# The latent attention's four projection tiles computed inside the loop over the directions' tables, and the shift's centre term from PSUM on ScalarE

## The chip, the cores and the metric

The kernel runs on one core of one Trainium2 chip. The metric is the time of one execution on the device in microseconds (us); lower is better. Engines: TensorE (PE in the profile; PEld is its weight load), VectorE (DVE), ScalarE (ACT), GpSimd (POOL) and SyncE (SP), which here only starts DMAs. ScalarE starts DMAs too.

## The reference, cut to what matters

The model is two hybrid layers (latent attention beside a bidirectional recurrence, then a mixture of experts) and a third block of another kind. Only the projection of the two hybrid layers is touched. For each layer li, on L = 1040 tokens (16 of them meta tokens) of width 1024:

```python
proj = h @ w_in[li]                                   # 1024 -> 448 + 1920 columns
c_q, c_kv, k_pe, rw = _split(proj, [256, 128, 64, 1920])
y_att = _mla(c_q, c_kv, k_pe, cos, sin, ...)          # rms norms of c_q and c_kv, rotation of k_pe
u = _centred_shift(rw, mu_prev, mu_next)              # p + mu_prev*(prev - p) + mu_next*(next - p)
r, k, v, wd_f, wd_b, ad_f, ad_b, gd = _split(u, [512, 512, 512, 64, 64, 64, 64, 128])
v = v + (v_first - v) * sigmoid(v0 + (v @ v1) @ v2)   # the second layer only
g = sigmoid(gd) @ g2
kk = k * k_k / sqrt(sum over a head of (k*k_k)**2 + 1e-12)
# per direction d: decay = exp(-exp(-softplus(-(w0 + tanh(wd) @ w2)) - 0.5)),
#                  a = sigmoid(a0 + ad @ a2),  kd = k * (1 + (a - 1) * k_a)
y_f, y_b = the recurrence over tokens of (r, decay, kd, v, kk, a), forward and reversed
```

## The kernel before, in words

**Tiles.** `proj` (L346) works with features on the 128 partitions and tokens along the free axis. One feature tile is 128 columns of `w_in` for all tokens (1040, padded to 1044). There are 19: fifteen of the recurrence (four of r, four of k, four of v, one each for wd, ad and gd), each of which goes through the centred shift, and four of the latent attention (two of c_q, one of c_kv, one of k_pe with its rotated copy), which do not. `ftile` makes one: it loads the weights (`load`, L357, on SyncE's queue), splits them into a high and a low part (ScalarE L251, VectorE L252), and issues 72 matmuls (three thirds of the tokens, eight pieces of the contraction, three products of the split, L256 to L258) into one PSUM buffer of three banks.

**Buffers.** PSUM has eight banks: the pool tag `mm` has two buffers of three banks each, the tag `tp` two of one bank. Projection tiles and the low-rank products of the loop both take `mm`; the transposes, the gate's products, the sums for the bonus and the sums of squares take `tp`. The weights' tiles, the evicted tile `pt` and the shifted tile `u` have two buffers each in SBUF.

**The shift.** `shifted` (L386 to L393) evicts the PSUM buffer with one ScalarE copy into `pt` (L390), multiplies by the centre coefficient on VectorE (L391), and adds the two neighbours with two more VectorE instructions (L392, L393). `plain` (L441, in `latent`) evicts without a shift (L444).

**Order.** The stage runs: the wd and ad tiles; `dirs`, which takes the four k tiles, forms the unit keys, and then loops over f = 0 to 3 (each: one r tile, then for both directions the decay and the gate of the keys from low-rank products L563, a scan L573, exponentials L576 and L577, and the products that fill two tables, AR and BK, L590 to L607, stored to DRAM at L610 from ScalarE's queue; then the sums for the bonus, L616). Behind the loop come the four v tiles, `values` (the residual of the second layer, L657 to L671; then for the forward and the reversed order of tokens nine transposes each, L684, a ScalarE copy L686 and a store L687), and `latent`: the rotated key, the gate's tile gd and its nine products, the key-value tile with its norm (reciprocal L495), the two q tiles, whose squares are summed over the features by 36 small matmuls (L513) for the rms norm. The products of other tiles are woven in by the `mid` hooks, called after a given third of a tile.

The kernel's instructions are put in order on each engine by a planner: it takes what is ready by its own model of the times, the earlier in the program first, and hands out buffers as they come free. Engines then run their queues in that order. DMAs signal through a small set of semaphores that are used in turn, so that a DMA can also wait for an earlier one with the same semaphore.

After the projection the recurrence `recur` starts: `r_fetch` loads pieces of AR and BK (L810, SyncE) and the first products are L825.

Of the kernel before, what the change touches and what calls it, by code (L numbers as in the profile page):

```python
# [10 lines left out]
F32 = mybir.dt.float32  # L11
# [4 lines left out]
AF = mybir.ActivationFunctionType  # L16
ALU = mybir.AluOpType
# [155 lines left out]
class K:  # L173
# [172 lines left out]
    def proj(self, li, hi, lo, p, S, psp, feed):  # L346

        nc, tc, I = self.nc, self.tc, self.I
        w = I["w_in"][li]
        with self.tpool(name="p_w", bufs=2) as wp, self.tpool(name="p_u", bufs=2) as up, \  # L350
# [34 lines left out]
            def shifted(j, u, mid={}):  # L385

                ps = ftile(own(j), early.pop(j, None), mid)
                pt = up.tile([128, TP + 1], F32, name="pt")
                nc.vector.memset(pt[:, 0:1], 0.0)
                nc.scalar.activation(pt[:, 1:].rearrange("p (q n) -> p q n", q=3), ps, AF.Copy)  # L390
                nc.vector.tensor_scalar(u, pt[:, 1:T + 1], p["c0"][:, j:j + 1], None, ALU.mult)  # L391
                nc.vector.scalar_tensor_tensor(u, pt[:, 0:T], p["mup"][:, j:j + 1], u, ALU.mult, ALU.add)  # L392
                nc.vector.scalar_tensor_tensor(u, pt[:, 2:T + 2], p["mun"][:, j:j + 1], u, ALU.mult, ALU.add)  # L393
                if self.dbg:
                    self.dbg(f"u{li}", (1920, T), u, lambda a: a[128 * j:128 * j + 128])
                return u
# [21 lines left out]

            wd = cp.tile([128, TP], F32, name="s_wd")
            ad = cp.tile([128, TP], F32, name="s_ad")  # L420
            for t in (wd, ad):
                nc.vector.memset(t[:, T:], 0.0)
            u = shifted(12, up.tile([128, T], F32, name="u"))
            nc.scalar.activation(wd[:, :T], u, AF.Tanh)
            shifted(13, ad[:, :T])
            lw = {}
            for nm in ("w2", "a2"):
                lw[nm] = cp.tile([128, RW], F32, name=f"r_{nm}")
                nc.sync.dma_start(lw[nm], I[f"rwkv_{nm}"][li].rearrange("d r f -> (d r) f"))
            with self.tpool(name="p_k", bufs=1) as kp:  # L430
                self.dirs(li, p, S, psp, up, kp, shifted, wd, ad, lw)
            with self.tpool(name="p_v", bufs=1) as vp:
                vt = [shifted(8 + f, vp.tile([128, T], F32, name=f"vt{f}", tag=f"val{f}")) for f in range(4)]
                self.values(li, vt, p, S, psp, up, vp)
                self.latent(li, p, S, psp, up, vp, shifted, ftile)

    def latent(self, li, p, S, psp, up, vp, shifted, ftile):

        nc = self.nc

        def plain(cols, mid=None):  # L441
            ps = ftile(cols, mid={2: mid} if mid else {})
            pt = up.tile([128, TP + 1], F32, name="pt")
            nc.scalar.activation(pt[:, :TP].rearrange("p (q n) -> p q n", q=3), ps, AF.Copy)  # L444
            return pt[:, :T]

        def c3(fn):
# [12 lines left out]
        nc.sync.dma_start(g2, self.I["rwkv_g2"][li])  # L460

        kr = plain([(384, 64, 0), (416, 32, 64), (384, 32, 96)])
        nc.gpsimd.tensor_tensor(kr[:64], kr[:64], cos[:64], ALU.mult)
        nc.gpsimd.tensor_tensor(kr[64:], kr[64:], sin[64:], ALU.mult)

        u = shifted(14, up.tile([128, T], F32, name="u"))
        gd = vp.tile([128, T], F32, name="gd")
        nc.scalar.activation(gd, u, AF.Tanh, scale=0.5)
        nc.vector.tensor_scalar(gd, gd, 0.5, 0.5, ALU.mult, ALU.add)

        def keys_end():
            ps = psp.tile([128, 3, 512], F32, name="kp_ps", tag="mm")
            c3(lambda q, c, n: nc.tensor.matmul(ps[:, q, :n], dup, kr[:, c:c + n], start=True, stop=True))
            b = vp.tile([128, T], F32, name="kp", tag="val3")
            c3(lambda q, c, n: nc.scalar.activation(b[:, c:c + n], ps[:, q, :n], AF.Copy))
            nc.scalar.dma_start(S["ckv"][1], b)


        ck = plain([(256, 128, 0)], keys_end)
        b = vp.tile([128, T], F32, name="ck_sq", tag="val2")  # L480
        nc.scalar.activation(b, ck, AF.Square)

        def gate_end():
            for c, n in TT:
                gp = psp.tile([128, 512], F32, name="g_ps", tag="tp")
                nc.tensor.matmul(gp[:n], gd[:, c:c + n], g2, start=True, stop=True)
                gs = vp.tile([128, RW], F32, name="g_sb", bufs=2)
                nc.scalar.activation(gs[:n], gp[:n], AF.Copy)
                nc.scalar.dma_start(S["g"][c:c + n, :], gs[:n])

        def ckv_end():
# [8 lines left out]
        sq = []  # L500
        for f, mid in enumerate((gate_end, ckv_end)):
            a = plain([(128 * f, 128, 0)], mid)
            x = vp.tile([128, T], F32, name=f"cq_sq{f}", tag=f"val{f}")
            nc.scalar.activation(x, a, AF.Square)
            sq.append(x)
            nc.vector.tensor_scalar(a, a, p["qn"][:, f:f + 1], None, ALU.mult)
            nc.scalar.dma_start(S["cq"][f], a)
        rq, nrq = S["rq"], S["nrq"]
        nc.vector.memset(rq, 1.0)
        sqs = psp.tile([128, 9, 2], F32, name="sqs", tag="tp")  # L510
        for i, (c, n) in enumerate(TT):
            for f in range(2):
                nc.tensor.matmul(sqs[:n, i], sq[f][:, c:c + n], ones[:, 0:2], start=f == 0, stop=f == 1)  # L513
        nc.scalar.activation(rq[:NM, 0:1], sqs[:NM, 0, 0:1], AF.Sqrt, scale=1.0 / 256, bias=self.eps["rms"][:NM])
        nc.scalar.activation(rq[:, 1:9], sqs[:, 1:9, 0], AF.Sqrt, scale=1.0 / 256, bias=self.eps["rms"])
# [4 lines left out]
    def dirs(self, li, p, S, psp, up, kp, shifted, wd, ad, lw):  # L520


        nc = self.nc
# [5 lines left out]
            nc.vector.tensor_scalar(rkp[:, f], self.pair, p["rk"][:, f:f + 1], None, ALU.mult)  # L529
        kt, kkt = [], []  # L530
        for f in range(4):
            k = shifted(4 + f, kp.tile([128, T], F32, name=f"k{f}"))
# [7 lines left out]
        for d in range(2):  # L540
            nc.gpsimd.memset(AR[d][:, 16 * d], 0.0)
        for f in range(4):
            r = shifted(f, up.tile([128, T], F32, name="u"), {} if f else {0: norms, 2: scaled})
            k, kk = kt[f], kkt[f][0]
            kds = []
            for d in range(2):
# [61 lines left out]
                for nm, t in (("AR", ar), ("BK", bk)):  # L608
                    for h in range(2):
                        nc.scalar.dma_start(S[nm][d][:, :, 2 * f + h], t[64 * h:64 * h + 64].rearrange("p c s t -> p c (s t)"))  # L610

            nc.vector.tensor_tensor(kds[0], kds[0], kds[1], ALU.add)
            nc.vector.tensor_tensor(kds[0], kds[0], r, ALU.mult)
# [1227 lines left out]
    def blocks(self, out, stop=None):  # L1841
        nc, tc = self.nc, self.tc
# [3 lines left out]
        for li in range(2):  # L1846
            for nm in ("AR", "BK"):
                S[nm] = [dt.tile([64, 17, 8, 128], F32, name=f"d_{nm}{li}{d}") for d in range(2)]
            S["cq"] = dt.tile([2, 128, T], F32, name=f"d_cq{li}")
            S["ckv"] = dt.tile([2, 128, T], F32, name=f"d_ckv{li}")  # L1850
            S["v"] = [dt.tile([T, RW], F32, name=f"d_v{li}{i}") for i in range(2)]
            S["g"] = dt.tile([T, RW], F32, name=f"d_g{li}")
            S["y"] = [dt.tile([T, RW], F32, name=f"d_y{li}{i}") for i in range(2)]
# [672 lines left out]
```

## Time and profile before

| | |
|---|---|
| Time of the kernel, median of 3 runs | 4419.15 us (4412.17 to 4427.49) |
| Profiled execution, its own time | 4422.43 us |
| Its span | 4420.6 us |
| TensorE busy | 3819.0 us (86%) |
| VectorE busy | 2765.4 us (63%) |
| ScalarE busy | 1846.1 us (42%) |
| GpSimd busy | 971.4 us (22%) |
| Mean granted TensorE clock | 0.902 |

A matmul's record in the trace is longer than the time until the next one can start, since they are pipelined; a stretch's busy time counts what is covered. A group's "idle before" is time in which its engine had nothing running just ahead of it, with what ended the wait. The granted clock is 1 at 2.4 GHz and 0.5 at 1.2 GHz.

### The profile page before, as it was taken

What the parts mean: (1) busy time and instruction counts of PE and PEld (TensorE: products, weight loads), DVE (VectorE), ACT (ScalarE), POOL (GpSimd) and SP (SyncE); (2) the same over time, 40 slices, a digit from 0 to 9 for tenths busy, and PEclk for the clock granted to TensorE, in tenths of its full rate; (3) what the DMA queues carried; (4) which work ended last, traced back from release to release, by engine and by line L of the source; (5) the groups of instructions that cost most, each with busy time, mean ns of one, the idle gap of its engine ahead of it and who ended that gap; (6) DMA issues with size and microseconds to landing.
All of it is one profiled execution on the core that took longest, in us unless ns stands there. A gap on an engine that the chain in (4) does not pass through costs nothing. (4 is left out here: it accounts for less than half of the span.)

```text
span 4420.6 us, 68400 instructions
## 1 busy us (share of the span) xinstructions
PE 3819.0 (86%) x27155; PEld 3149.8 (71%) x27155; DVE 2765.4 (63%) x4684; ACT 1846.1 (42%) x3007; POOL 971.4 (22%) x671
## 2 busy tenths in 40 slices
PE   7887797889699688896877987998898899999998
PEld 7587676777576486675767866676786677888787
DVE  7852768757698857526667667898645743332354
ACT  4322344642387643232445532886424532111232
POOL 2331114301342234211133012331422320000000
PEclk9888798999799887786988998999898899999999
DMA  4446564113499824446642043998521131111232
GB/s 153 100 131 176 146 155 124 41 50 137 164 343 349 309 83 105 110 143 152 166 132 62 1 162 115 337 336 307 204 71 31 36 113 58 44 47 48 86 122 88
DMA packets 386203, 611.95 MB, mean 138 GB/s; under 512 B 50467, under 2 KB 217603, under 8 KB 383811
## 3 DMA queue, kind: packets, MB, share of 16 engines
q1 hardware_dynamic: 283650, 493.90, 36.0%
q10 hardware_dynamic: 85200, 70.97, 5.4%
q0 software_dynamic: 17024, 42.62, 3.1%
q8 instruction: 216, 3.54, 0.3%
q14 instruction: 113, 0.92, 0.1%
HBM read 491.65 MB, written 123.45 MB: 139 GB/s over the span
## 5 line engine op out<-in xcount | busy, mean ns | idle before, releaser
L252 DVE TENSOR_TENSOR w13l<-xw,w13h 128x1024 fp32r<-128x1024 f32 x248 | 296.2, 1219 | 55.9 <-ACT w13h L251 54.6
L251 ACT ACTIVATE w13h<-xw 128x1024 fp32r<-128x1024 f32 x256 | 267.4, 1058 | 128.3 <-PE x_hp L258 73.3
L256 PE MATMUL pp_ps<-T_hi,pw_hi 128*128 128x348 f32 x912 | 310.2, 341 | 6.3 <-ACT ta L565 2.4
L257 PE MATMUL pp_ps<-T_lo,pw_hi 128*128 128x348 f32 x912 | 306.0, 336 | 1.4 <-DVE T_lo L1760 1.3
L258 PE MATMUL pp_ps<-T_hi,pw_lo 128*128 128x348 f32 x912 | 304.9, 334 | 0.0
L2417 PE MATMUL f_mm<-F_hi,f_wh 128*128 128x512 f32 x704 | 222.9, 398 | 1.7 <-ACT F_hi L251 1.7
L2417 PE MATMUL f_mm<-F_lo,f_wh 128*128 128x512 f32 x704 | 222.6, 397 | 0.0
L2417 PE MATMUL f_mm<-F_hi,f_wl 128*128 128x512 f32 x704 | 222.4, 397 | 0.0
L256 PE MATMUL x_hp<-w13h,x_h 128*96 128x512 f32 x512 | 207.3, 405 | 0.2 <-ACT x_h L251 0.2
L257 PE MATMUL x_hp<-w13l,x_h 128*96 128x512 f32 x512 | 203.6, 398 | 0.0
L258 PE MATMUL x_hp<-w13h,x_l 128*96 128x512 f32 x512 | 202.6, 396 | 0.0
L825 PE MATMUL aa<-ar_p,bk_p 64*128 64x128 f32 x1088 | 131.0, 368 | 73.2 <-DMA bk_p<-d_BK 41.5
L256 PEld LDWEIGHTS pp_ps<-T_hi,pw_hi 128*128 128x128 f32 x912 | 180.2, 198 | 19.5 <-issue 7.8
L257 PEld LDWEIGHTS pp_ps<-T_lo,pw_hi 128*128 128x128 f32 x912 | 180.4, 198 | 5.1 <-DVE T_lo L1760 2.6
L258 PEld LDWEIGHTS pp_ps<-T_hi,pw_lo 128*128 128x128 f32 x912 | 180.1, 197 | 3.0 <-issue 3.0
L252 DVE TENSOR_TENSOR f_wl<-F_raw,f_wh 128x1024 fp32r<-128x1024 f32 x44 | 53.7, 1222 | 203.0 <-ACT f_wh L251 203.0
L287 POOL TENSOR_TENSOR g_x<-g_x,g2g 128x1024 f32<-128x1024 f32 x6 | 14.3, 2388 | 750.6 <-ACT g_x L284 750.6
L251 ACT ACTIVATE f_wh<-F_raw 128x1024 fp32r<-128x1024 f32 x44 | 46.4, 1060 | 307.2 <-PE f_mm L2417 301.5
L825 PEld LDWEIGHTS aa<-ar_p,bk_p 64*128 64x128 f32 x1088 | 110.2, 257 | 88.9 <-issue 44.3
L1619 POOL DMA_INDIRECT d_y<-x_o,r_idx x64 | 104.8, 1638 | 311.0 <-DVE x_al L252 289.4
L827 DVE TENSOR_TENSOR A<-aa,cmask 128x512 f32<-128x512 f32 x136 | 87.2, 682 | 131.2 <-PE aa L825 131.2
L2417 PEld LDWEIGHTS f_mm<-F_hi,f_wh 128*128 128x128 f32 x704 | 133.2, 189 | 34.4 <-ACT F_hi L251 2.0
(627 smaller groups left out, 11225.2 us busy)
## 6 DMA issues: line engine op xcount, KB each, us to landing
xw<-in_moe_w SPq DMA_DIRECT2D x256, 512.0 KB
xw<-in_moe_w SPq DMA_DIRECT2D x64, 1024.0 KB
wd_raw<-in_w_down SPq DMA_DIRECT2D x44, 512.0 KB
pw_raw<-in_w_in SPq DMA_DIRECT2D x36, 512.0 KB
d_AR<-AR ACTq DMA_DIRECT2D x32, 544.0 KB
d_BK<-BK ACTq DMA_DIRECT2D x32, 544.0 KB
ar_p<-d_AR SPq DMA_DIRECT2D x68, 256.0 KB
bk_p<-d_BK SPq DMA_DIRECT2D x68, 256.0 KB
```

Source lines behind the costliest of these rows:

```text
L251: nc.scalar.activation(hi, src, AF.Copy)
L252: (lo_eng or nc.vector).tensor_tensor(lo, src, hi.bitcast(F32), ALU.subtract)
L256: mm(out, wh, xh, start=first, stop=False)
L257: mm(out, wh, xl, start=False, stop=False)
L258: mm(out, wl, xh, start=False, stop=last)
L287: e1.tensor_tensor(out[:n], out[:n], gb[:n], ALU.mult)
L825: nc.tensor.matmul(aa[d][:, h - z], bk[q, h], ar[q, h], start=True, stop=True)
L827: nc.vector.tensor_tensor(A[d][:, z:z + 4], aa[d], R["mask"][d][:, None, :].to_broadcast([128, 4, 128]), ALU.mult)
L1619: nc.gpsimd.indirect_dma_start(out=y2[:, :], out_offset=bass.IndirectOffsetOnAxis(ap=si, axis=0), in_=y, in_offset=None, bounds_check=2 * ...
L2417: nc.tensor.matmul(p[:, j], a[:, k], b[:, k, 512 * j:512 * j + 512], start=st, stop=sp)
```

## The change: what it does

Three edits.

1. The four tiles of the latent attention move out of `latent` into a new generator, `compressed`, which is stepped once in each pass of the loop of `dirs`, behind the first direction's table stores. Its first two steps make the q tiles: evict, square (into a `u` buffer), sum the squares with 18 matmuls each into a `tp` buffer, copy the sums to the small tile `cqs`, scale, and store to `S["cq"]` as before. The third and fourth steps make the key-value tile and the rotated-key tile and store them raw to a new DRAM tile, `S["raw"]`, from ScalarE's queue.
2. `latent` loads the two raw tiles back (SyncE), rotates and norms them, and makes the gate's tile with the norm's and the rotation's products as its `mid` hooks; the gate's products follow. The q norm's factors come from the sums in `cqs`.
3. In `shifted`, the centre term is a second ScalarE activation that reads PSUM with the centre coefficient as its scale, in place of the VectorE instruction L391. The tiles that it writes are padded to 1044.

```diff
@@ shifted
                 nc.scalar.activation(pt[:, 1:].rearrange("p (q n) -> p q n", q=3), ps, AF.Copy)
-                nc.vector.tensor_scalar(u, pt[:, 1:T + 1], p["c0"][:, j:j + 1], None, ALU.mult)
+                nc.scalar.activation(u.rearrange("p (q n) -> p q n", q=3), ps, AF.Copy, scale=p["c0"][:, j:j + 1])
+                u = u[:, :T]
                 nc.vector.scalar_tensor_tensor(u, pt[:, 0:T], p["mup"][:, j:j + 1], u, ALU.mult, ALU.add)
...
@@ proj
-                self.dirs(li, p, S, psp, up, kp, shifted, wd, ad, lw)
+                self.dirs(li, p, S, psp, up, kp, shifted, wd, ad, lw, self.compressed(p, S, psp, up, cp, ftile))
...
+    def compressed(self, p, S, psp, up, cp, ftile):
...
+        S["cqs"] = cqs = cp.tile([128, 2, 9], F32, name="cqs")
+        for f in range(2):
+            a = plain([(128 * f, 128, 0)])
+            x = up.tile([128, TP], F32, name="u")[:, :T]
+            nc.scalar.activation(x, a, AF.Square)
+            sqs = psp.tile([128, 9, 2], F32, name="sqs", tag="tp")
+            for i, (c, n) in enumerate(TT):
+                nc.tensor.matmul(sqs[:n, i], x[:, c:c + n], self.ones32[:, 0:2], start=True, stop=True)
+            nc.scalar.activation(cqs[:NM, f, 0:1], sqs[:NM, 0, 0:1], AF.Copy)
+            nc.scalar.activation(cqs[:, f, 1:9], sqs[:, 1:9, 0], AF.Copy)
+            nc.vector.tensor_scalar(a, a, p["qn"][:, f:f + 1], None, ALU.mult)
+            nc.scalar.dma_start(S["cq"][f], a)
+            yield
+        for i, cols in enumerate(([(256, 128, 0)], [(384, 64, 0), (416, 32, 64), (384, 32, 96)])):
+            nc.scalar.dma_start(S["raw"][i], plain(cols))
+            yield
...
@@ latent
-        kr = plain([(384, 64, 0), (416, 32, 64), (384, 32, 96)])
+        ck, kr = (vp.tile([128, T], F32, name=nm) for nm in ("ck", "kr"))
+        nc.sync.dma_start(ck, S["raw"][0])
+        nc.sync.dma_start(kr, S["raw"][1])
...
+        u = shifted(14, up.tile([128, TP], F32, name="u"), {0: norm, 1: rotated})
...
-        sqs = psp.tile([128, 9, 2], F32, name="sqs", tag="tp")
-        for i, (c, n) in enumerate(TT):
-            for f in range(2):
-                nc.tensor.matmul(sqs[:n, i], sq[f][:, c:c + n], ones[:, 0:2], start=f == 0, stop=f == 1)
...
+        nc.vector.tensor_tensor(cqs[:, 0, 1:9], cqs[:, 0, 1:9], cqs[:, 1, 1:9], ALU.add)
...
@@ dirs, in the loop over the directions, behind the table stores
+                if d == 0:
+                    next(between)
```

## Rows read from the trace of the kernel before

**Rows 1.** The page's first part: busy us, share of the span, instructions.
```profile
PE 3819.0 (86%) x27155; PEld 3149.8 (71%) x27155; DVE 2765.4 (63%) x4684; ACT 1846.1 (42%) x3007; POOL 971.4 (22%) x671
```
**Rows 2.** Busy time by stretches: loop, tail, start of the recurrence, in both layers.
```profile
core 0: us, PE busy (x) PEld busy (x) DVE busy (x) ACT busy (x) POOL busy (x), PEclk, DMA share, GB/s
...
126.00:284.00 158.00, 124.12 (x500) 96.31 (x499) 132.54 (x122) 55.83 (x64) 78.60 (x47) 0.76 0.50 123
284.00:398.40 114.40, 114.36 (x700) 107.41 (x699) 29.59 (x28) 36.27 (x53) 16.56 (x12) 0.99 0.40 129
398.40:405.10 6.70, 0.00 (x0) 0.03 (x1) 6.70 (x4) 0.40 (x2) 0.76 (x2) 0.62 0.83 271
1663.00:1821.00 158.00, 127.20 (x490) 95.64 (x490) 128.58 (x118) 53.65 (x62) 75.10 (x47) 0.73 0.48 119
1821.00:1969.00 148.00, 142.45 (x754) 119.86 (x754) 45.82 (x43) 45.84 (x69) 16.07 (x13) 0.90 0.34 105
1969.00:1975.60 6.60, 0.01 (x1) 0.00 (x1) 5.88 (x5) 0.41 (x2) 0.00 (x0) 0.50 0.98 304
```
**Rows 3.** Groups by line in the first loop: busy us, mean ns, idle before, releasers.
```profile
L563 PE MATMUL low_ps<-s_ad,r_a 64*128 64x348 f32 x48 | 25.5, 688 | 7.9 <-ACT pt L390 7.9
...
L563 PE MATMUL low_ps<-s_wd,r_w 64*128 64x348 f32 x48 | 21.6, 598 | 5.8 <-ACT lg L565 5.8
...
L252 DVE TENSOR_TENSOR pw_lo<-pw_raw,pw_hi 128x1024 fp32r<-128x1024 f32 x5 | 6.0, 1206 | 5.1 <-ACT pw_hi L251 5.1
...
L251 ACT ACTIVATE pw_hi<-pw_raw 128x1024 fp32r<-128x1024 f32 x5 | 5.3, 1052 | 22.1 <-issue 21.6 <-PE pp_ps L257 0.5
...
L391 DVE TENSOR_SCALAR u<-pt,pc 128x1040 f32<-128x1040 f32 x4 | 3.8, 952 | 0.0
```
**Rows 4.** Waits in the first loop: us in total, times, longest.
```profile
POOL BK L548 <- DMA d_BK<-BK: 15.9, 6, 6.4
...
PE low_ps L563 <- ACT pt L390: 7.9, 2, 6.8
...
PE low_ps L563 <- ACT lg L565: 5.8, 2, 5.4
```
**Rows 5.** Timeline: evictions of two successive tiles; a low-rank product at full clock.
```profile
307.16 1.03 ACT L390 ACTIVATE pt<-pp_ps 128x1044 f32<-128x1044 f32 x1
...
318.64 1.03 ACT L390 ACTIVATE pt<-pp_ps 128x1044 f32<-128x1044 f32 x1
...
197.57 2.02 PE L563 MATMUL low_ps<-s_wd,r_w 64*128 64x348 f32 x6
```
**Rows 6.** Groups by line in the first tail, 284 to 398.4 us.
```profile
L495 DVE RECIPROCAL ck_sq<-ck_sq 128x1040 f32<-128x1040 f32 x1 | 6.7, 6653 | 0.9 <-ACT ck_sq L494 0.9
...
L513 PE MATMUL sqs<-ones,cq_sq 128*128 128x2 f32 (+1 forms) x36 | 3.9, 242 | 0.0
...
L463 POOL TENSOR_TENSOR pt<-pt,cos 64x1040 f32<-64x1040 f32 x1 | 3.3, 3302 | 24.2 <-DMA cos<-rope 24.2
```
**Rows 7.** VectorE's timeline: the last value tile, layer 0 and layer 1.
```profile
322.04 1.30 DVE L393 SCALAR_TENSOR_TENSOR vt<-pt,pcol,vt 128x1040 f32<-128x1040 f32 x1
...
1896.10 1.24 DVE L670 SCALAR_TENSOR_TENSOR vf<-vsg,vf 128x1040 f32<-128x1040 f32 x1 [3.74 <-ACT vsg L666]
```
**Rows 8.** ScalarE's timeline: the first value copies; the last value stores.
```profile
327.17 1.07 ACT L686 ACTIVATE v_sb<-v_ps 16x512 f32<-16x512 f32 x2 [7.49 <-PE v_ps L684]
...
366.94 0.98 ACTq L687 DMA_DIRECT2D d_v<-v_sb  x2
...
1937.85 0.81 ACTq L687 DMA_DIRECT2D d_v<-v_sb  x2
```
**Rows 9.** Timeline at the start of the recurrence: SyncE's first load, TensorE's first product.
```profile
395.87 1.14 SPq L810 DMA_DIRECT2D ar_p<-d_AR  x2
...
405.10 0.76 PE L825 MATMUL aa<-ar_p,bk_p 64*128 64x128 f32 x2 [6.74 <-DMA bk_p<-d_BK]
```
**Rows 10.** Waits in SyncE's queue, 376 to 420 us: us in total, times, longest.
```profile
SPq L810 <- DMA d_cq<-pt: 4.5, 1, 4.5
```

More of the change, by code (lines that the diff above doesn't have):

```diff
@@ L420, in proj @@
             ad = cp.tile([128, TP], F32, name="s_ad")
-            for t in (wd, ad):
-                nc.vector.memset(t[:, T:], 0.0)
-            u = shifted(12, up.tile([128, T], F32, name="u"))
+            nc.vector.memset(wd[:, T:], 0.0)
+            u = shifted(12, up.tile([128, TP], F32, name="u"))
             nc.scalar.activation(wd[:, :T], u, AF.Tanh)
-            shifted(13, ad[:, :T])
+            shifted(13, ad)
             lw = {}
@@ L430, in proj, with plain @@
             with self.tpool(name="p_k", bufs=1) as kp:
-                self.dirs(li, p, S, psp, up, kp, shifted, wd, ad, lw)
+                self.dirs(li, p, S, psp, up, kp, shifted, wd, ad, lw, self.compressed(p, S, psp, up, cp, ftile))
             with self.tpool(name="p_v", bufs=1) as vp:
-                vt = [shifted(8 + f, vp.tile([128, T], F32, name=f"vt{f}", tag=f"val{f}")) for f in range(4)]
+                vt = [shifted(8 + f, vp.tile([128, TP], F32, name=f"vt{f}", tag=f"val{f}")) for f in range(4)]
                 self.values(li, vt, p, S, psp, up, vp)
                 self.latent(li, p, S, psp, up, vp, shifted, ftile)
-    def latent(self, li, p, S, psp, up, vp, shifted, ftile):
+    def compressed(self, p, S, psp, up, cp, ftile):
         nc = self.nc
-        def plain(cols, mid=None):
-            ps = ftile(cols, mid={2: mid} if mid else {})
+        def plain(cols):
+            ps = ftile(cols)
             pt = up.tile([128, TP + 1], F32, name="pt")
@@ L445, in plain, with latent @@
             return pt[:, :T]
+        S["cqs"] = cqs = cp.tile([128, 2, 9], F32, name="cqs")
[14 more added lines that the diff above has]
+            yield
+    def latent(self, li, p, S, psp, up, vp, shifted, ftile):
+        nc = self.nc
         def c3(fn):
@@ L460, in latent, with norm @@
         nc.sync.dma_start(g2, self.I["rwkv_g2"][li])
-        kr = plain([(384, 64, 0), (416, 32, 64), (384, 32, 96)])
+        ck, kr = (vp.tile([128, T], F32, name=nm) for nm in ("ck", "kr"))
+        nc.sync.dma_start(ck, S["raw"][0])
+        nc.sync.dma_start(kr, S["raw"][1])
         nc.gpsimd.tensor_tensor(kr[:64], kr[:64], cos[:64], ALU.mult)
         nc.gpsimd.tensor_tensor(kr[64:], kr[64:], sin[64:], ALU.mult)
[L466 to L479, printed above, removed]
         b = vp.tile([128, T], F32, name="ck_sq", tag="val2")
         nc.scalar.activation(b, ck, AF.Square)
[L483 to L491, printed above, removed]
+        def norm():
             ps = psp.tile([128, 3, 512], F32, name="ck_ps", tag="mm")
@@ L497, in ckv_end @@
             nc.scalar.dma_start(S["ckv"][0], ck)
[L500 to L508, printed above, removed]
-        nc.vector.memset(rq, 1.0)
@@ L510, in latent, with rotated @@
-        sqs = psp.tile([128, 9, 2], F32, name="sqs", tag="tp")
-        for i, (c, n) in enumerate(TT):
-            for f in range(2):
-                nc.tensor.matmul(sqs[:n, i], sq[f][:, c:c + n], ones[:, 0:2], start=f == 0, stop=f == 1)
-        nc.scalar.activation(rq[:NM, 0:1], sqs[:NM, 0, 0:1], AF.Sqrt, scale=1.0 / 256, bias=self.eps["rms"][:NM])
-        nc.scalar.activation(rq[:, 1:9], sqs[:, 1:9, 0], AF.Sqrt, scale=1.0 / 256, bias=self.eps["rms"])
+        def rotated():
+            ps = psp.tile([128, 3, 512], F32, name="kp_ps", tag="mm")
+            c3(lambda q, c, n: nc.tensor.matmul(ps[:, q, :n], dup, kr[:, c:c + n], start=True, stop=True))
+            k2 = vp.tile([128, T], F32, name="kp", tag="val3")
+            c3(lambda q, c, n: nc.scalar.activation(k2[:, c:c + n], ps[:, q, :n], AF.Copy))
+            nc.scalar.dma_start(S["ckv"][1], k2)
@@ new lines, in latent @@
+        u = shifted(14, up.tile([128, TP], F32, name="u"), {0: norm, 1: rotated})
+        gd = vp.tile([128, T], F32, name="gd")
+        nc.scalar.activation(gd, u, AF.Tanh, scale=0.5)
+        nc.vector.tensor_scalar(gd, gd, 0.5, 0.5, ALU.mult, ALU.add)
+        for c, n in TT:
+            gp = psp.tile([128, 512], F32, name="g_ps", tag="tp")
+            nc.tensor.matmul(gp[:n], gd[:, c:c + n], g2, start=True, stop=True)
+            gs = vp.tile([128, RW], F32, name="g_sb", bufs=2)
+            nc.scalar.activation(gs[:n], gp[:n], AF.Copy)
+            nc.scalar.dma_start(S["g"][c:c + n, :], gs[:n])
@@ L516, in latent @@
+        rq, nrq, cqs = S["rq"], S["nrq"], S["cqs"]
+        nc.vector.memset(rq, 1.0)
+        nc.vector.tensor_tensor(cqs[:NM, 0, 0:1], cqs[:NM, 0, 0:1], cqs[:NM, 1, 0:1], ALU.add)
+        nc.vector.tensor_tensor(cqs[:, 0, 1:9], cqs[:, 0, 1:9], cqs[:, 1, 1:9], ALU.add)
+        nc.scalar.activation(rq[:NM, 0:1], cqs[:NM, 0, 0:1], AF.Sqrt, scale=1.0 / 256, bias=self.eps["rms"][:NM])
+        nc.scalar.activation(rq[:, 1:9], cqs[:, 0, 1:9], AF.Sqrt, scale=1.0 / 256, bias=self.eps["rms"])
         nc.vector.reciprocal(rq, rq)
@@ L518, in latent, with dirs @@
         nc.vector.tensor_scalar(nrq, rq, -1.0, None, ALU.mult)
-    def dirs(self, li, p, S, psp, up, kp, shifted, wd, ad, lw):
+    def dirs(self, li, p, S, psp, up, kp, shifted, wd, ad, lw, between):
         nc = self.nc
@@ L531, in dirs @@
         for f in range(4):
-            k = shifted(4 + f, kp.tile([128, T], F32, name=f"k{f}"))
+            k = shifted(4 + f, kp.tile([128, TP], F32, name=f"k{f}"))
             kk = kp.tile([128, T], F32, name=f"kk{f}")
@@ L542, in dirs @@
         for f in range(4):
-            r = shifted(f, up.tile([128, T], F32, name="u"), {} if f else {0: norms, 2: scaled})
+            r = shifted(f, up.tile([128, TP], F32, name="u"), {} if f else {0: norms, 2: scaled})
             k, kk = kt[f], kkt[f][0]
@@ L1850, in blocks @@
             S["ckv"] = dt.tile([2, 128, T], F32, name=f"d_ckv{li}")
+            S["raw"] = dt.tile([2, 128, T], F32, name=f"d_raw{li}")
             S["v"] = [dt.tile([T, RW], F32, name=f"d_v{li}{i}") for i in range(2)]
```

## The prediction

> **What bounds the kernel now.** The page's first part comes first [rows 1]: TensorE is busy for 86% of the span, VectorE for 63%. That is a mean over stages, so the next view is the busy time by stretches around the change, for both layers [rows 2]. Each layer has a loop over the directions' tables (126 to 284 us, and 1663 to 1821 us) and behind it a tail with nine projection tiles, up to the first product of the recurrence. The reader should see two different limits. In the loop TensorE is busy 124.1 of 158 us at a mean granted clock of 0.76 (1 is its level of 2.4 GHz, 0.5 that of 1.2), while VectorE is at 132.5: the loop is a chain through VectorE, ScalarE and GpSimd, and TensorE has 33.9 us idle (30.8 in layer 1). In the first tail TensorE is busy 114.36 of 114.4 us at clock 0.99, VectorE only 29.6: TensorE is the bound. The short third stretch has no TensorE work and DMAs at 0.83 and 0.98.
>
> The waits inside the loop come next [rows 4]: the low-rank products wait for ScalarE to empty a PSUM buffer (7.9 and 5.8 us), and GpSimd waits 15.9 us for the table BK to be written out. Last, the end of the tail [rows 9]: the first product of the recurrence starts at 405.10 after 6.74 us of idle, and SyncE's loads there had waited 4.5 us for the store of the second q tile [rows 10].
>
> **What leaves the tail.** One projection tile takes 11.5 us of TensorE at full clock: its successive evictions start at 307.16 and 318.64 [rows 5]. Four of the nine move, 46 us. The sums of squares go too (36 matmuls, 3.9 us [rows 6]), so 49.9 us of TensorE leaves each tail. If TensorE stayed the bound, 114.4 would become 64.5 us. It does not: another chain is late next.
>
> Layer 0: the fourth value tile is shifted by 322.04 + 1.30 = 323.34 [rows 7]. The centre term costs 1.03 us on ScalarE [rows 5] in place of a VectorE step of 0.95 us in the loop [rows 3] and, I take it, less where GpSimd is still: 323.6. The first pair of value rows was copied at 327.17 after waiting 7.49 us for TensorE, which had projection tiles in between [rows 8]. Without them it can start at 324.2, 3 us sooner (0.6 us for the first transposes, an estimate from the 2.02 us of a low-rank product [rows 5], which has more columns). The 18 copies then run over two buffers with a store behind each; I keep the pace of before, so the last store, which ended at 367.92, ends at 364.9. Could they be quicker without the projection in between? TensorE's share was a third of it at most; I leave that for the range.
>
> The other chains fit beneath. The forward half of the copies is through at about 344. Then the rotated key needs its table load (taken as the 4.7 us from load to use that come below), two GpSimd products of some 3 us each [rows 6], a small product and copies: about 357. The key norm has a 6.65 us reciprocal [rows 6] and some 6 us around it: also about 357. The gate's tile is projected by 335 and its nine products fit between the value transposes.
>
> From the first table load to the first product it took 405.10 - 395.87 = 9.2 us, of which 4.5 was the wait for the q store [rows 9, 10]. That store is now long done, so 4.7 us remain: 364.9 + 4.7 = 369.6, against 405.1. **The tail gains 35.5 us.**
>
> Layer 1: behind its value tiles stands the residual, four passes with one buffer each. The last of them stood 3.74 us waiting for a ScalarE result that TensorE, busy with projection tiles, had delivered late [rows 7]. This wait goes; the rest of the chain stays. The last store ended at 1937.85 + 0.81 = 1938.66 [rows 8], now 1934.9, plus 4.7: 1939.6. Before, the first product came with the end of the third stretch, at 1975.6 [rows 2]. **Gain 36.0 us.**
>
> **What it costs in the loop.** TensorE gets the 49.9 us. Bounds: if all idle time of TensorE is filled and its clock stays, the loop grows by 49.9 - 33.9 = 16.0 us (19.1 in layer 1). If nothing is filled, by 49.9. If the clock goes to full, it may grow by nothing: a low-rank product of three matmuls took 2.02 us at full clock [rows 5], 16 of them 32 us, where these lines were busy 25.5 + 21.6 [rows 3]; with the projections and the rest in proportion TensorE's 124.1 becomes about 100, plus 49.9 still below 158.
>
> The other engines in the loop. VectorE: four more splits at 1.21 us, two scalings of the form of the centre term, less four centre terms at 0.95 [rows 3]: +2.9 us in 158. ScalarE: four splits at 1.05, four evictions and four centre terms at 1.03, two squares about as long: +14.5 us, on 55.8 busy [rows 2, 3, 5]. ScalarE has room, but it is in order: a new eviction that waits for TensorE holds the next exponential, for which VectorE and GpSimd stand. The moved DMAs (four weight loads on SyncE; two q stores and two new raw stores on ScalarE's queue, in front of the table stores) add about 4 MB in each layer by their shapes, against DMAs at 0.50 [rows 2]. All lie beside VectorE's work; if that cover goes, ScalarE's 14.5 us is the largest of them, and is what would bring +16 to +30.
>
> I take the 16.0 and 19.1: filled idle is the usual case for tiles whose weights are in SBUF, and the higher clock and ScalarE's delays pull to opposite sides.
>
> The centre term outside the loop: 11 other shifted tiles per layer trade at most 0.95 us on VectorE for 1.03 on ScalarE. There TensorE is the bound with 11.5 us a tile, against some 3 us of ScalarE: nothing either way, 0 to 0.3 us for a tile whose shift is waited for.
>
> Sum: -35.5 - 36.0 + 16.0 + 19.1 = -36.4 us. The profiled execution took 4422.4 us, 3.3 above the median of the three runs (4419.15), so **4386 on its own scale and 4383 on the median's.**
>
> **The rivals.** *The loop swallows it for nothing.* TensorE, denser, keeps the full clock, and the recurrence, which needs only the tables, starts beneath the value stores. For it: the clock in the loop was 0.76, and the first products wait for PSUM and tables that are free by about 357 to 360. Against: SyncE's queue and the SBUF of the value tiles. Time: 16 to 19 us a layer back, up to 10 more by the early start: 4350 as the middle, 4335 to 4367. The Trainium skill (TensorE: Matmul & The Clock Gate, the section on the HAM clock gate) says that the throttled state is the default and that activity releases it; by that rule alone the lengthening is zero, and the sum 4419 - 71 = 4348. The rows agree in direction, 0.76 in the loop beside 0.99 in the dense tail [rows 2].
>
> *Half of the gaps stay.* The idle 33.9 us is made of waits for evictions and for VectorE; if the new tile fills only half, the loop grows by about 33 us and a layer gains 0 to 10: 4399 to 4419.
>
> *Slower: the two PSUM buffers.* Projection tiles and low-rank products share two three-bank buffers. A tile that holds one for 11.5 us and then for two copies (2.1 us) leaves one buffer for the four low-rank products of a pass; if the second direction's products always come behind it, each pass pays up to 13.6 us, 54 us a loop and 58 with the sums of squares: 22 us a layer lost, 4463. It decides from 9 us a pass, where the loop eats the tail's 36. For it: the waits on evictions [rows 4]. Against: before the change TensorE did a tile of 72 matmuls in each pass with the same two buffers, and paid 13.7 us of such waits in all four [rows 4]. [...]
>
> *The tiles are not computed in the loop at all*, since the planner orders by readiness: they could pile up behind it and stand in front of the value tiles. Then nothing moves; it is in the "half" case.
>
> **How the numbers follow.** The forecast has 0.52 (loop longer by 10 to 26 us, 4367 to 4399), the free loop 0.15, half of the gaps 0.20, the PSUM buffers 0.13. Within 0.3% (13 us) nothing can be told from no change. Faster than 4406: the forecast, the free loop and a quarter of the third case, 0.72; slower than 4432: 0.13; between, 0.15. The range that leaves out a tenth on either side is 4342 to 4424.
>
> **What would show it.** Right: windows over the loop with TensorE busy near 170 us in about 175 and a higher clock; a tail of about 86 us from the last table to the first product of the recurrence, with TensorE idle a third of it and the value stores as its last chain; no wait for the q store in SyncE's queue. Wrong: a loop of over 190 us (158 now), low-rank products waiting for evictions far longer than these 13.7 us; or a tail that still ends with the gate or the key norm rather than the value stores.

## The result and the profile after

The changed kernel takes **4458.2 us** (median of 4 runs, 4456.56 to 4466.16) against 4417.88 of the kernel before beside it (4 runs): ratio 1.009, 95% interval [1.0076, 1.0104], 40 us slower. The forecast was 4383. Its profiled execution has a span of 4456.4 us, 35.8 more than before.

Busy time by stretches, same columns as [rows 2]: loop and tail of layer 0, then of layer 1. The bounds moved with the work: a loop ends with the last bonus product, a tail with the recurrence's first product. The loop of layer 1 is counted here from its first key-norm product, some 12 us earlier in the work than in [rows 2].

```profile
core 0: us, PE busy (x) PEld busy (x) DVE busy (x) ACT busy (x) POOL busy (x), PEclk, DMA share, GB/s
126.00:337.00 211.00, 175.62 (x819) 148.81 (x819) 133.38 (x126) 71.13 (x83) 75.88 (x47) 0.80 0.44 109
337.00:436.40 99.40, 76.89 (x378) 61.22 (x377) 25.95 (x21) 33.87 (x48) 20.95 (x19) 0.83 0.57 181
1687.90:1899.80 211.90, 184.72 (x877) 153.27 (x877) 130.89 (x127) 75.93 (x89) 71.58 (x47) 0.82 0.44 108
1899.80:2027.20 127.40, 101.47 (x425) 71.45 (x425) 40.40 (x33) 42.20 (x64) 20.92 (x19) 0.80 0.43 134
```

The first loop grew from 158 to 211 us. TensorE's busy time in it grew by 51.5 (124.12 to 175.62), and its idle time is 35.4 where it was 33.9: **in this kernel none of the idle was filled.** The tail shrank from 121.4 us to 99.4, not to 86, with TensorE idle for 22.5 of it.

Waits in the first loop (us in total, times, longest), to be held against [rows 4]:

```profile
POOL BK L557 <- DMA d_BK<-BK: 73.5, 6, 14.9
...
DVE cum L582 <- POOL lg L579: 22.9, 5, 7.3
...
PE low_ps L572 <- ACT pt L445: 19.2, 3, 7.5
...
PE low_ps L572 <- ACT u L391: 6.2, 4, 2.2
```

GpSimd waits 73.5 us for BK's stores (15.9 before), the scan waits for GpSimd, and the low-rank products for evictions of projection tiles 25.4 us (13.7 for evictions before). One half pass (one direction in one pass of the loop) shows how these hang together: GpSimd's timeline, then ScalarE's. The tile lg holds a low-rank product after its eviction by ScalarE; GpSimd scales it, and the scan that makes the decay reads it.

```profile
219.83 3.47 POOL L599 TENSOR_TENSOR BK<-kd,cum 128x1024 f32<-128x1024 f32 x2
237.03 0.20 POOL L557 MEMSET BK<- 128x128 f32 x1 [13.73 <-DMA d_BK<-BK]
237.20 1.06 POOL L579 TENSOR_SCALAR lg<-lg 128x1044 f32<-128x1044 f32 x1
```
```profile
225.77 1.39 ACTq L619 DMA_DIRECT2D d_BK<-BK  x1
...
227.20 2.41 ACTq L619 DMA_DIRECT2D d_BK<-BK  x1
229.66 1.06 ACT L251 ACTIVATE pw_hi<-pw_raw 128x1024 fp32r<-128x1024 f32 x1 [3.36 <-PE low_ps L572]
230.63 1.02 ACT L390 ACTIVATE pt<-pp_ps 128x1044 f32<-128x1044 f32 x1
231.55 1.12 ACT L391 ACTIVATE u<-pp_ps,pc 128x1044 f32<-128x1044 f32 x1
232.69 1.28 ACT L574 ACT_TABLE_LOAD   x1
233.98 1.13 ACT L574 ACTIVATE lg<-low_ps,phalf 128x1044 f32<-128x1044 f32 x1
```

The eviction of lg stands behind the issue of BK's stores, a weight split, a tile's two evictions and a table load. Then lg, in SBUF at 235.1, is scaled only at 237.20, because the clearing of BK's first block is in front of it in GpSimd's queue and there is one BK buffer, whose store lands at 237.0. From eviction to scaling lg waited 20.1 us in layer 0 and 9.0 in layer 1 (sums over eight half passes, from the timelines), nearly all of it behind the clear. Before it had waited 14 us in each, in layer 0 mostly behind BK products that GpSimd was computing, in layer 1 half behind the clear. So these sums alone do not price the clear; an experiment below does. The scans now follow each other by 26 to 28.5 us from the third half pass on (183.1, 211.6, 238.3, 265.8, 292.1, 319.6); before it was 14 to 22.5 there.

The end of the tail, on TensorE, then ScalarE, then SyncE (a wait in its queue, and an issue), where [rows 8, 9, 10] are those of before:

```profile
417.66 1.38 PE L695 MATMUL v_ps<-ident,vr 128*128 128x128 f32 x5
419.69 8.48 PE L514 MATMUL g_ps<-g,gd 128*16 128x512 f32 x12 [0.65 <-ACT v_sb L697]
...
436.36 0.79 PE L836 MATMUL aa<-ar_p,bk_p 64*128 64x128 f32 x2 [1.94 <-DMA bk<-d_BK]
```
```profile
420.71 0.32 ACTq L698 DMA_DIRECT2D d_v<-v_sb  x1
421.61 0.59 ACT L516 ACTIVATE g_sb<-g_ps 16x512 f32<-16x512 f32 x1 [0.93 <-PE g_ps L514]
```
```profile
SPq L1009 <- DMA d_g<-g_sb: 20.8, 2, 18.7
```
```profile
430.03 2.99 SPq L821 DMA_DIRECT2D bk<-d_BK  x2
```

The last value store comes 84 us behind the last bonus product (forecast 81.2). But the gate's nine products start only then, and take to 434.4, held by their copies. The wait for the q store is gone from SyncE's queue there, as forecast. In its place the loads there wait 20.8 us for the gate's stores, and the load of BK that ends TensorE's last wait, at 436.36, is issued behind them.

### The profile page after: what moved, and what is told of

It reads as the page before. It is cut to its first block, busy times and chain, and to the rows that moved or that the text cites. A ratio compares the mean times of both kernels' runs of the same rounds, so it can differ in the third digit from the quotient of the medians.

```text
span 4456.4 us, 68461 instructions
## 1 busy us (share of the span) xinstructions
PE 3840.5 (86%) x27155; PEld 3160.8 (71%) x27155; DVE 2738.9 (61%) x4656; ACT 1884.8 (42%) x3049; POOL 969.4 (22%) x671
## 5 line engine op out<-in xcount | busy, mean ns | idle before, releaser
L252 DVE TENSOR_TENSOR w13l<-xw,w13h 128x1024 fp32r<-128x1024 f32 x248 | 296.4, 1220 | 51.5 <-ACT w13h L251 47.8
```

The costliest lines, as they stand in the source:

```text
L252: (lo_eng or nc.vector).tensor_tensor(lo, src, hi.bitcast(F32), ALU.subtract)
```

## The experiments

Theories: **A**, the tile's matmuls in front of the second direction's low-rank products lengthen the loop; **B**, the clear of BK in GpSimd's queue does; **C**, the third edit (centre term on ScalarE) does; **D**, in the tail the copies wait for stores, with two buffers for the stored rows. Loop and tail below are read from each profiled execution: from the first key-norm product (L640, which writes kk_ps) to the end of the last bonus product (L627), and from there to the first product of the recurrence; layer 0 / layer 1. The time of before was measured again beside each group of runs (medians of 4416.0 to 4417.9), and each ratio is to the one beside it.

| run | median us | ratio to before, interval | loop | tail |
|---|---|---|---|---|
| before | 4417 | | 168.8 / 169.9 | 121.4 / 154.5 |
| after | 4458.2 | 1.009 [1.0076, 1.0104] | 221.8 / 211.9 | 99.4 / 127.4 |
| e1 centre alone | 4450.6 | 1.0077 [1.006, 1.0094] | 178.5 / 177.7 | 123.7 / 152.1 |
| e2 centre back | 4442.8 | 1.0059 [1.0042, 1.0076] | 207.7 / 209.3 | 98.4 / 128.3 |
| e3 clear late | 4423.5 | 1.0005 [0.9994, 1.0015] | 196.8 / 200.9 | 99.8 / 128.6 |
| e4 tile behind | 4490.7 | 1.0163 [1.0146, 1.018] | 226.5 / 221.4 | 113.2 / 135.5 |
| e5 before, clear late | 4415.6 | 0.9994 [0.9985, 1.0004] | 164.1 / 168.5 | 122.3 / 151.2 |
| e6 e1, clear late | 4423.4 | 1.0011 [1.0001, 1.002] | 167.0 / 166.5 | 121.8 / 150.9 |
| e7 gate first | 4468.6 | 1.0111 [1.0094, 1.0127] | 223.4 / 224.0 | 96.5 / 121.2 |
| e8 clear late, gate first | 4417.2 | 0.9998 [0.9989, 1.0008] | 198.2 / 197.7 | 96.7 / 120.3 |
| e9 e3, four store buffers | 4391.4 | 0.9945 [0.9928, 0.9961] | 198.2 / 191.3 | 82.7 / 118.0 |
| e10 e8, four store buffers | 4402.4 | 0.9968 [0.9954, 0.9983] | 198.2 / 201.1 | 90.1 / 115.4 |
| e11 e9, issue on SyncE | 4379.5 | 0.9908 [0.9888, 0.9927] | 186.4 / 188.9 | 84.4 / 119.7 |
| e12 before, clear late, four | 4417.4 | 1.0000 [0.9989, 1.0011] | 165.7 / 168.8 | 120.8 / 151.3 |
| e13 e3, few matmuls | 4373.8 | 0.9898 [0.9881, 0.9915] | 181.9 / 176.6 | 96.6 / 127.4 |
| e14 before, e11's three mends | 4419.8 | 1.0007 [0.9998, 1.0016] | 165.5 / 163.6 | 121.9 / 154.0 |
| e15 e11, centre back | 4361.1 | 0.9879 [0.9863, 0.9894] | 182.5 / 183.6 | 81.8 / 118.1 |

What the profiled executions do outside these four stages, where only the third edit changes anything (six shifted tiles ahead of each loop), takes 3788 to 3815 us in the 17 runs; a median can differ from the sum of a row by that much.

### The third edit by itself

e1 is the kernel before with only this edit; e2 is the kernel after without it:

```diff
-                nc.vector.tensor_scalar(u, pt[:, 1:T + 1], p["c0"][:, j:j + 1], None, ALU.mult)
+                nc.scalar.activation(u.rearrange("p (q n) -> p q n", q=3), ps, AF.Copy, scale=p["c0"][:, j:j + 1])
```

> The kernel before with only the third edit: the centre term as a second ScalarE activation out of PSUM. Theory A (the projection tile in front of the second direction's low-rank products costs the loop its 54 us), theory B (GpSimd's clearing of BK, queued in front of the scaling of lg, waits for BK's store) : this edit is worth nothing here, within 6 us of before (4412 to 4424). Theory C (the second reader of the PSUM buffer and ScalarE's extra microsecond a tile are what holds the loop): at least half of the loss is here, 4435 or more.

> The kernel after with the third edit undone (centre term on VectorE again). Theories A and B: the loss stays, 4452 to 4466. Theory C: it goes by half or more, 4440 or less.

e1 came out as theory C had it, +33 us (its profiled execution was the fastest of its four, and its four stages are 17 us longer than before's); e2 gave back only 15 of 40, neither theory's number. GpSimd's waits for BK's store in e1's first loop:

```profile
POOL BK L548 <- DMA d_BK<-BK: 34.1, 5, 12.8
```

Twice the 15.9 of before, with nothing of BK edited. In two half passes of the first loop (clears at 218.97 and 258.99) the clear now stands in front of the scaling of lg where it had stood behind it. The planner, which orders by its own times, had turned the two round. So A, B and C are not exclusive: the order on GpSimd had to be fixed before the edit could be weighed.

### The clear, and the tile's place

e3 makes the clear depend on kd, so that it stands directly in front of the first BK product; e4 steps the generator behind the second direction's low-rank products:

```diff
@@ e3
-                nc.gpsimd.memset(bk[:, 16 * d], 0.0)
...
+                bk = kp.tile([128, 17, 2, 64], F32, name="BK")
+                nc.gpsimd.tensor_scalar(bk[:, 16 * d].rearrange("p s t -> p (s t)"), kd[:, 0:128], 0.0, None, ALU.mult)
                 both(lambda o, s: nc.gpsimd.tensor_tensor(o, s[0], s[1], ALU.mult), bk, 1 - d, (rv(kd), cum))
@@ e4
                 low(ad, lw["a2"], ta, p[f"a0{d}h"][:, f:f + 1])
+                if d:
+                    next(between)
...
-                if d == 0:
-                    next(between)
```

> The kernel after; the first block of BK is cleared by an instruction that reads kd, so that it stands directly in front of the first BK product and no longer in front of the scaling of lg. Order of TensorE unchanged. Theory B: GpSimd's 73.5 us of waits for BK's store in the first loop leave the chain that leads to the scan, some 35 to 45 us a layer of the 54 come back: 4370 to 4395. Theory A: the tile still stands in front of the second direction's products; at most 10 us a layer: 4438 to 4458.

> The kernel after; the generator is stepped behind the second direction's low-rank products instead of behind the first direction's stores, so that both directions' products stand together on TensorE, as before the change, and two projection tiles together. BK is cleared as in the kernel after. Theory A: the half passes go back to about 17 us where no tile stands in front, 30 to 40 us a layer come back: 4380 to 4400. Theory B: the clearing still waits for the store in front of lg; at most 10 us a layer: 4438 to 4458.

e3 took 35 us off the kernel after: 25 from the first loop and 11 from the second. That is close to the 20.1 + 9.0 us for which lg had waited. Theory B holds for that part, though it came to less than it forecast. In the half pass that was shown above, GpSimd now scales lg as soon as ScalarE delivers it, and the wait for the store is gone:

```profile
228.33 1.06 POOL L578 TENSOR_SCALAR lg<-lg 128x1044 f32<-128x1044 f32 x1 [8.37 <-issue]
```

Both theories missed e4: it is 32 us slower than after. Both directions' products stood together, and the second scan followed the first by 13.4 us, but the next pass's first scan came 34 to 46 us later, behind two tiles instead of one. GpSimd in e4:

```profile
237.93 0.20 POOL L557 MEMSET BK<- 128x128 f32 x1 [13.13 <-DMA d_BK<-BK]
253.42 1.06 POOL L579 TENSOR_SCALAR lg<-lg 128x1044 f32<-128x1044 f32 x1 [15.28 <-ACT lg L574]
```

So A in its first form (the place between the two directions is what costs) is not borne out: the other place costs more. What was left of it, the tile's time in series with the tables wherever it stands, is e13's question.

### Is the order of GpSimd all of the third edit's price?

e5 and e6 are the kernel before and e1, both with e3's edit.

> The kernel before with only the late clearing of BK (as in the third experiment). Theory B': in the kernel before, the clear stood in front of the scaling of lg in few half passes, and waited 15.9 us in the first loop; 0 to 8 us a layer come back: 4400 to 4418. If the planner's order of the rest changes with it, it can go either way by the same amount.

> The centre term on ScalarE alone (as in the first experiment, which cost 33 us) with the late clearing of BK. Theory B' (the edit itself is nearly free, and its cost was that the clear got in front of the scaling of lg in more half passes: 34.1 us of waits against 15.9): the time of the fifth experiment within 6 us. Theory C (the PSUM buffer is held longer, ScalarE is in the way): 20 us or more above the fifth experiment.

e6 is 27 us faster than e1 and 8 above e5: of the 33 us, theory B' explains about 25, and theory C at most 8. Where the 8 lie is not shown: the four stages of e5 and e6 add up to the same (606.1 and 606.2 us). e5 itself changes nothing that can be told.

### The tail

e7 makes the gate's tile and products first; e8 adds e3's edit:

```diff
+                self.gate(li, S, psp, up, vp, shifted)
                 vt = [shifted(8 + f, vp.tile([128, TP], F32, name=f"vt{f}", tag=f"val{f}")) for f in range(4)]
...
-        u = shifted(14, up.tile([128, TP], F32, name="u"), {0: norm, 1: rotated})
+        norm()
+        rotated()
```

> The kernel after with the gate's tile and its nine products in front of the four value tiles, so that they run between the value tiles' matmuls. If the tail was long because the gate's products stood behind all the value transposes (from the last of these to the first product of the recurrence 17.4 us in layer 0, 15.0 in layer 1): 10 to 15 us a layer come back, 4428 to 4438. If the tail is bound by TensorE or by the value stores, which start 11.5 us later here: 5 us or less, 4448 to 4460.

> The kernel after with both: the late clearing of BK and the gate in front of the value tiles. If the two costs are independent, the sum of the two gains: about 4395 to 4403, faster than the kernel before.

The gate went in between the value tiles' matmuls, and the tail still gained only 2.9 and 6.2 us. In e7 the second loop became 12 us longer as well, with no edit in it, so that e7 missed both expectations; e8 missed by 14 us. A loop without an edit can thus differ by 12 us between two profiled executions. e3's 25 us in the first loop are well clear of that, its 11 in the second are not by themselves; the medians, 35 us apart, bear out the sum. TensorE at the end of e7's first tail:

```profile
434.05 1.02 PE L702 MATMUL v_ps<-ident,vr 128*16 128x128 f32 x4 [2.09 <-ACT v_sb L704]
436.02 0.79 PE L843 MATMUL aa<-ar_p,bk_p 64*128 64x128 f32 x2 [0.94 <-ACT v_sb L704]
```

Now the value rows are last, held by their copies. e9 (on e3) and e10 (on e8) therefore give the stored rows four buffers:

```diff
-                vs = vp.tile([128, RW], F32, name="v_sb", bufs=2)
+                vs = vp.tile([128, RW], F32, name="v_sb", bufs=4)
...
-            gs = vp.tile([128, RW], F32, name="g_sb", bufs=2)
+            gs = vp.tile([128, RW], F32, name="g_sb", bufs=4)
```

> The third experiment (after, BK cleared late) with four buffers instead of two for the value rows and the gate's rows that are stored. Theory D (in the shortened tail the copies wait for the landing of the stores two rows earlier, 13.3 + 6.9 us in the first layer's tail of the third experiment, and through them the gate's products): 8 to 18 us a layer come back, 4388 to 4407. If the pace is set by the two PSUM buffers and the order instead: within 6 us of the third experiment, 4417 to 4430.

> The eighth experiment (late clear, gate in front of the value tiles) with four buffers for the stored rows. There the 18 value copies waited 19.0 us for stores in the first layer and ran from 372 to 414. Theory D: the tail becomes 12 to 18 us shorter a layer, 4383 to 4395. If not, 4411 to 4424.

Theory D holds in e9: 32 us, of which 17 in the first tail and 11 in the second. (The second loop, which the edit does not touch, is 9.6 us shorter too.) Waits for stores in the first tail of e3, then of e9:

```profile
ACT v_sb L698 <- DMA d_v<-v_sb: 13.3, 8, 4.7
...
ACT g_sb L516 <- DMA d_g<-g_sb: 6.9, 4, 2.2
```
```profile
ACT v_sb L698 <- DMA d_v<-v_sb: 4.8, 4, 3.4
...
ACT g_sb L516 <- DMA d_g<-g_sb: 0.5, 1, 0.5
```

20.2 us of waits became 5.3. e10 came out above its range, 11 us behind e9. Its tails are 7.4 us longer and 2.6 shorter than e9's, so with four buffers the gate is at least no worse where the change put it; most of the rest is the second loop, where the two do not differ in their edits.

### ScalarE's queue, and what the change is worth at all

e11 is e9 with the table stores issued by SyncE; e12 and e14 put these mends (the edits of e3, e9 and, in e14, e11) on the kernel before, without the change:

```diff
-                        nc.scalar.dma_start(S[nm][d][:, :, 2 * f + h], t[64 * h:64 * h + 64].rearrange("p c s t -> p c (s t)"))
+                        nc.sync.dma_start(S[nm][d][:, :, 2 * f + h], t[64 * h:64 * h + 64].rearrange("p c s t -> p c (s t)"))
```

> The ninth experiment with the table stores issued from SyncE's queue instead of ScalarE's. In the third experiment the issue of BK's store held ScalarE 2.3 to 3.3 us in most half passes just in front of the evictions that lead to lg. If that is on the chain of the loop: 10 to 18 us a layer under the ninth. If the loop is held by the tile's matmuls in front of the low-rank products: at most 4 us a layer. If SyncE's queue holds weight loads behind the stores: slower than the ninth.

> The kernel before with the late clear and the four store buffers. Its first tail is bound by TensorE (busy 114.36 of 114.4 us), so the buffers should be worth nothing: within 6 us of the fifth experiment, 4408 to 4420. If the end of its tail is held by the stores, up to 10 us a layer less.

> The kernel before with the three mends of the eleventh experiment (late clear, four store buffers, table stores from SyncE's queue), without the change. If the gain of the eleventh experiment (4379) belongs to the change once its waits are gone: 4400 to 4418 here. If the mends alone bring it: 4375 to 4390.

e11 gained another 12 us: its loops are shorter by 11.8 and 2.4 us, the first as the one expectation had it and the second as the other. ScalarE, then SyncE, in one of its half passes:

```profile
238.64 1.06 ACT L251 ACTIVATE pw_hi<-pw_raw 128x1024 fp32r<-128x1024 f32 x1 [8.46 <-PE pp_ps L257]
239.60 1.02 ACT L445 ACTIVATE pt<-pp_ps 128x1044 f32<-128x1044 f32 x1
241.08 1.13 ACT L573 ACTIVATE lg<-low_ps,phalf 128x1044 f32<-128x1044 f32 x1 [0.46 <-PE low_ps L571]
```
```profile
237.22 3.27 SPq L620 DMA_DIRECT2D d_BK<-BK  x2
240.98 3.16 SPq L357 DMA_DIRECT2D pw_raw<-in_w_in  x1
```

The 3.27 us of issue now lie beside ScalarE's evictions. In e9 these issues had held ScalarE's queue for 26.9 us in the first loop and 24.0 in the second. The Trainium skill (Trainium Kernel Development and Optimization, Key Constraints) says that issuing from another engine saves only the issue time, since all queues share the same DMA engines. The trace agrees: the gains stay below that issue time, and the DMAs were busy for as long, 0.54 of 176.6 us in e11's first loop and 0.51 of 188.6 in e9's. But the gain is no larger than the 12 us by which a loop without an edit differed in e7. That it comes from the issue is likely, and not shown.

On the kernel before, the same mends are worth nothing (e12; e14, 2 us above its range), so the 38 us by which e11 is under it belong to the change once its waits are out of the way.

### What is left of the loop's lengthening

e13 is e3 with 18 instead of 72 matmuls in each moved tile (two of eight slices of the sum, so the latent attention's inputs are not those of the reference); e15 is e11 with e2's edit.

```diff
-            ps = ftile(cols)
+            ps = ftile(cols, ks=2)
```

> The third experiment (after, BK cleared late), with only 18 of the 72 matmuls of each of the four moved tiles (two of eight slices of the sum; the latent attention's inputs are wrong for it, nothing else changes: loads, splits, evictions and stores stay). Theory A (the tile's time on TensorE in front of the low-rank products is what is left of the loop's lengthening, 28 us in layer 0 and 31 in layer 1): the loop goes back to within 8 us of the kernel before's, 4365 to 4378. Rival (the additional evictions on ScalarE, the PSUM buffers, the weight splits): at most 10 us a layer, 4403 to 4420.

> The eleventh experiment with the third edit undone (centre term on VectorE). By the difference of the sixth and the fifth experiment (8 us) the third edit costs a little even without the clear in the way: 4368 to 4376. If VectorE is on the chain of the loop (four r tiles at 0.95 us a layer, and the key tiles before it): 4380 to 4390.

The tile's matmuls are most of what is left: without three quarters of them the change would cost the loop 13.1 and 6.7 us instead of e3's 28.0 and 31.0, and the time fell by 50 us, into the range expected (though the first loop stayed 13 us, not 8, above that of before). The first loop, from 126 to its last bonus product, of e3, e13, e11 and e15:

```profile
126.00:311.80 185.80, 172.05 (x819) 145.40 (x818) 134.87 (x127) 72.96 (x86) 83.50 (x48) 0.83 0.51 127
...
126.00:298.80 172.80, 145.41 (x629) 118.52 (x627) 139.81 (x127) 74.95 (x89) 86.39 (x48) 0.79 0.54 137
...
126.00:302.60 176.60, 166.75 (x825) 141.56 (x823) 134.65 (x127) 74.68 (x87) 84.49 (x48) 0.88 0.54 134
...
126.00:298.10 172.10, 161.24 (x828) 137.74 (x826) 136.53 (x131) 70.06 (x83) 84.56 (x48) 0.91 0.56 138
```

e13 takes 26.6 us of TensorE's work out of e3's loop; 13.0 shorten it, and the rest comes back as idle time. Theory A's second form, the tile in series with the chain, is therefore not shown alone. Its rival is that e3's loop is bound by TensorE itself, which idles there for only 13.8 of 185.8 us; no run parts the two.

**Once the waits are gone, the idle is filled.** TensorE idles 9.9 us in e11's first loop, where it idled 33.9 before the change and 35.4 after it.

e15 is the fastest, 4361.1 us, 1.2% under the kernel before and 18 us under e11, more than the 3 to 11 expected. Its loop does the work of the kernel after with TensorE idle for 10.9 us instead of 35.4, and in 161 us of TensorE instead of 176, at clock 0.91 instead of 0.80.

## Why the prediction was wrong

Working through its steps, in profiled us, layer 0 / layer 1:

| step | forecast | after | e11 |
|---|---|---|---|
| tail | -35.5 / -36.0 | -22.0 / -27.1 | -37.0 / -34.8 |
| loop | +16.0 / +19.1 | +53.0 / +42.0 | +17.6 / +19.0 |

**The work was counted rightly, and the waits were not.** TensorE's 49.9 us arrived in the loop as 51.5. The value stores ended 84 us behind the tables for 81.2 forecast. With three waits removed each term comes within 2 us of the forecast, and the time (4379.5 for 4383) within 4. That is in part luck. In e11's first loop 9.9 us of idle are left, not none, but TensorE is busy for only 42.6 us more, not 49.9, at a clock of 0.88 (0.76 before). In its tails the last value store is issued 75.6 and 112.3 us behind the loop (forecast 81.2 and 113.8), and 8.7 and 7.4 us go from there to the first product (forecast 4.7), still with the gate's products in them.

**The step that failed first: "filled idle is the usual case".** The prediction took 16.0 and 19.1 us for the loops, with all idle filled. It had its other bound in hand, 49.9 us if nothing is filled, and the first loop paid 53, the second 42. The idle time was that in which TensorE waited for a chain, and the added work lengthened the chain as it came. In the first loop the largest part that an experiment singles out is the order on GpSimd, 25 us (e3); three quarters of the tiles' matmuls come next, 15 us (e13). In front of the eviction of lg, ScalarE has the stores' issue (e11, likely) and the added evictions, which were not tried by themselves. With the clear and the issue out of the way the same idle was filled, 33.9 us to 9.9, so what failed is not that idle can be filled but that nothing in the chain was priced as standing behind the new work. The prediction had read GpSimd's 15.9 us wait for BK's store [rows 4] and then given it no price. It costed ScalarE's 14.5 us as lying beside VectorE's work and named its loss of cover, but not BK's clear, which needed only a slightly later lg to get in front of it.

**"Nothing either way" for the centre term.** Its durations were nearly right (1.12 us on ScalarE for the 1.03 forecast) and its price was not: +33 us alone, about 25 of them through the clear's place in GpSimd's queue.

**"The gate's nine products fit between the value transposes".** They started behind the last of them, and the 4.7 us from the last store to the first product became 15.3 (421.03 to 436.36). Moving them in front did not mend it (e7). What helped was more buffers for stored rows (e9), which shortened the copies; the gate's products stayed behind them. On the kernel before, the same buffers are worth nothing (e12).

**The rivals.** The time lies 5 us from that of the rival with the two PSUM buffers, but for the most part through other waits. Its sign test, low-rank products waiting far longer than 13.7 us, shows 25.4, and a loop of over 190 us was named as what would prove the forecast wrong, and so was a tail that ends with the gate. But its place was the second direction's products behind the tile, and putting them in front of it (e4) made things worse. The free loop fell: the granted clock rose from 0.76 to 0.80 only. So did the half of the gaps, since none was filled, and the tiles left behind the loop: the first loop has 819 matmul records where it had 500.

**Still open:** why the third edit costs 18 us in the mended kernel (e11, whose six runs span 4366 to 4389, against e15: 9 in the loops, 4 in the tails, the rest unplaced), where it cost 8 at most in e6; and how much of the loop's growth is the issue, the evictions and the plain work of TensorE. The two evictions hold a tile's PSUM buffer a microsecond longer, which was not tried by itself.

## What to carry to other kernels

Idle time of an engine in a stage bound by a chain is filled only as far as the new work does not hold up the chain; look at which queue, buffer and eviction the new work takes in front of the chain, and price the wait that is already visible there (a store with one buffer, 15.9 us) as if it stood first. When a planner sets the order, a microsecond on one engine can move an instruction on another, and a loop without an edit can move by 12 us (e7): compare the order of every queue before weighing an edit, and pin the dangerous instruction by its data. Where a stage stops being TensorE-bound, look for the double buffers whose latency TensorE used to hide.

## What the runs showed of the hardware

The two DMAs of 544 KB each for BK held the issuing engine's queue for 1.2 to 5.5 us (1.39 + 2.41 in the half pass above, 3.27 on SyncE in e11, 5.47 in e4), while a 256 KB store of 128 value rows took 0.33 us to issue; and BK's buffer was free only 9.8 us after the second issue began (227.20 to 237.03). The granted clock of the first loop was low where TensorE idled much: 0.71 in e1 (44.0 of 168.4 us idle), 0.76 before (33.9 of 158), 0.80 after (35.4 of 211). It was higher where TensorE idled little: 0.88 in e11 (9.9 of 176.6) and 0.91 in e15 (10.9 of 172.1). From after to e15 the same matmuls took 14 us less (175.62 to 161.24). The row of e1:

```profile
126.00:294.40 168.40, 124.42 (x491) 96.15 (x490) 130.49 (x115) 59.74 (x68) 77.50 (x47) 0.71 0.54 115
```
